# Summing one block's weighted expert rows on the tensor engine throughout, with the next block's expert rows begun earlier

## The chip, the cores and the metric

One Trainium2 chip, one core of it. The metric is the device time of one execution in microseconds. The kernel before was run three times: 1658.19, 1659.23 and 1664.06 us, median 1659.23 us.

## The reference, cut to what matters

512 tokens of 1024 features pass one decoder layer. The mixing sub-layer (sparse attention over a shared latent beside a gated linear recurrence, one output projection, a layer norm) gives `h`. The change is in the second sub-layer, which picks 16 of 16384 single-neuron experts for each of 8 heads, so 128 experts for each token, from the scores of two lists of 128 sub-keys, and sums their rows of `v`:

```python
def one_block(xb):                        # 128 tokens
    q = (xb @ w_q).reshape(PEER_BLOCK, PEER_HEADS, 2, PEER_KEY_DIM // 2)
    s = jnp.einsum('thpd,hpkd->thpk', q, sub_keys)
    s_top, i_top = lax.top_k(s, K)
    ...
    best, pos = lax.top_k(cand.reshape(PEER_BLOCK, PEER_HEADS, K * K), K)
    experts = jnp.take_along_axis(cand_idx.reshape(...), pos, axis=-1)
    g = jax.nn.softmax(best, axis=-1)
    h = jax.nn.gelu(jnp.einsum('td,thkd->thk', xb, u[experts]))
    return jnp.einsum('thk,thkd->td', g * h, v[experts])
```

The result is `LayerNorm(alpha * h + ffn)`. Everything is float32.

## The kernel before, in words

The 512 tokens are four blocks of 128, a token on each partition. **Blocks 2 and 3** are worked densely: all 16384 experts are streamed through the tensor engine, and a matrix `G` holds each token's weight for each expert (zero for most). **Blocks 0 and 1** fetch only the rows that their tokens chose: a "row" here is one indirect DMA that gathers, for each of the 128 tokens, its k-th expert's 1024 features (512 KB, one instruction on the GpSimd queue, `gather`, L625 to L629), and what is then done with it. Each of the two blocks has 128 rows of `u` (a dot product with `h` on VectorE, L651; after every 32 of them a gelu on ScalarE and a product give the weights) and then 128 rows of `v`, which are weighted and summed into the block's tile `hs[b]`.

The program has these stages. `stage([0])` does the mixing layer and the expert choice (`queries`) for block 0. `stage([1, 2, 3])` does the same for the other three blocks: projections (L189, L204), `select` (L416, L417), the recurrence `hgrn` block by block, `attention` block by block, `mix_norm` (L486), `queries` (sub-key scores on TensorE, L518 and L522; the 16 best of each list on VectorE, L532 to L565; `routing`, L567 on, which turns places into expert numbers and weights). Then `dense` builds `G` in 64 steps of four tokens (one-hot tiles on VectorE, L735, and ScalarE, L739; products on TensorE, L744; copies on ScalarE, L722), and loops over 128 groups of experts (`into_hidden`, `weigh`, `out_of_hidden`, L771 and L791).

The rows of blocks 0 and 1 are a background stream. `peer_gather(b)` (L645) is a Python generator that emits one row at each step; `pump(n)` (L693) takes n steps of the first generator in the list `todo`. The stages call `pump` at many places, with the numbers in `PUMP`: in `stage([1, 2, 3])` before 206 rows are asked for, against 204 that the generator of block 0 has. Tile's scheduler then fixes each engine's order when the program is built: it takes what is ready, and among that what comes first in the program. The VectorE instructions of the rows keep their order among themselves. The gathered rows share a ring of four tiles (`GB`).

Block 0's rows of `v` are split. The first 76 are summed on VectorE, each with one instruction that multiplies by the weight and adds to `hs[0]` (L664). The other 52 are summed on TensorE by `pe_gather` (L672 to L688): ScalarE makes a diagonal matrix `dg` of the weights (one tile, L680), two matmuls multiply it with the two halves of the row into two PSUM banks (L682; a float32 matmul shows as two passes, so a row has four), and VectorE adds the banks to `hs[0]` at the end (L687). 14 of the 52 come after the queries of the second stage (`PEK1`), 8 before `G` is built and 30 during its building (`PEK2`, `PEPRE`). Block 1's 256 rows are all on VectorE and begin with the building of `G`: one at every third step (22), the other 234 spread over the 128 groups of the dense loop.

```python
PUMP = {"cw": 4, "qi": 4, "hf": 4, "hq": 4, "hi": 4, "hg": 3, "qa": 2, "hgrn": 1, "att": 4, "mix": 1, "sel": 2,
        "q0": 7, "q1": 0, "q2": 0, "q3": 0}
...
    stage([0], xT0)
    todo.append(peer_gather(0))
    stage([1, 2, 3], consts_loaded["xT1"])
    todo.append(peer_gather(1))
```

Of the kernel before, what the change touches and what calls it, by code (L numbers as in the profile page):

```python
# [24 lines left out]
DENSE = (2, 3)  # L25
# buffers of the rings of tiles
HGB = 5
GB = 4
UB = 4
# [5 lines left out]
# rows of experts worked off at each such place of the program (sel: one at every second step)  # L35
PUMP = {"cw": 4, "qi": 4, "hf": 4, "hq": 4, "hi": 4, "hg": 3, "qa": 2, "hgrn": 1, "att": 4, "mix": 1, "sel": 2,
        "q0": 7, "q1": 0, "q2": 0, "q3": 0}
# rows of block 0's sum that the tensor engine takes: after the queries, and beside the dense weights
PEK1 = 14
PEK2 = 38  # L40
PEPRE = 8
PEG = 60
# tokens of each four whose weights ScalarE multiplies in
GACTS = (3, 4)
# a row of experts at every so manyth group of the dense weights
GPUMP = 3
# the dense step by which all rows are worked off
# [4 lines left out]
def tile_decoder_layer(ctx, tc, a, out):  # L52
# [70 lines left out]
    def layer_norm(ys, os_, g, b, nm):  # L123
        """Each y is a tile or a list of its parts along the features."""
        n = len(ys)
        mv = cst.tile([128, n, 2], F32, name="mv" + nm, tag="ln_mv", bufs=2)
        parts = [y if isinstance(y, list) else [y[:, k * 512:(k + 1) * 512] for k in range(2)] for y in ys]
        for i in range(n):
            st = cst.tile([128, 2, 6], F32, name=f"st{nm}_{i}", tag="ln_st", bufs=2)
            for k in range(2):  # L130
                nc.vector.bn_stats(st[:, k, :], parts[i][k])  # L131
            nc.vector.bn_aggr(mv[:, i, :], st)
        ve = cst.tile([128, n], F32, name="ve" + nm, tag="ln_ve", bufs=2)
        nc.vector.tensor_scalar(ve, mv[:, :, 1], EPS, None, op0=ALU.add)
        r = rsqrt(ve, n, nm)
        for i, o in enumerate(os_):
            if isinstance(ys[i], list):
                for k in range(2):
                    sl = slice(k * 512, k * 512 + 512)
                    nc.vector.scalar_tensor_tensor(o[:, sl], parts[i][k], mv[:, i, 0:1], g[:, sl],  # L140
                                                   op0=ALU.subtract, op1=ALU.mult)
            else:
                nc.vector.scalar_tensor_tensor(o, ys[i], mv[:, i, 0:1], g, op0=ALU.subtract, op1=ALU.mult)  # L143
            nc.vector.scalar_tensor_tensor(o, o, r[:, i:i + 1], b, op0=ALU.mult, op1=ALU.add)  # L144
# [34 lines left out]
    def tok_major(blocks, xT, w, name):  # L179
        """x W for each block, tokens on partitions."""  # L180
        ps_ = [bank(f"{name}{b}") for b in blocks]
        n = w.shape[-1]
        step = 2 if n == 512 else 4
        for k0 in range(0, 8, step):
            wt = stream(f"{name}w{blocks[0]}_{k0}", w[:, k0:k0 + step, :])
            pump(PUMP[name])
            for i in range(len(blocks)):
                for k in range(step):
                    nc.tensor.matmul(ps_[i][:, :n], xT[:, k0 + k, i * 128:(i + 1) * 128], wt[:, k, :],  # L189
                                     start=(k0 + k == 0), stop=(k0 + k == 7))  # L190
        return ps_

    def feat_major(blocks, xT, w, name):
        """(x W)^T for all blocks at once, features on partitions: a bank for each 128 features."""
# [23 lines left out]
    def lower_bound():  # L218
# [7 lines left out]
        # lower bound of the forget gate: f = fa + fc * tanh(z / 2)  # L226
# [42 lines left out]
    def hgrn(b, pr, mixT):  # L269
# [42 lines left out]
        # the states before each chunk of 32  # L312
# [87 lines left out]
    def select(b, pr):  # L400
        """What to add to the negated attention scores of the keys that the index doesn't choose."""
# [91 lines left out]
    def queries(blocks, hT):  # L493
        """Sub-key scores and, for each of the 16 lists, its 16 best."""
# [13 lines left out]
        for g in range(4):  # L508
# [15 lines left out]
            for i, b in enumerate(blocks):  # L524
# [13 lines left out]
                if g >= 2 and i < len(later):  # L538
                    routing(later[i], 0, *r[later[i]])
            if g == 1:  # L540
                later = sorted(blocks, key=lambda b: (b not in DENSE, b))
                if blocks == [0]:
                    routing(later.pop(0), 0, *r[0])
            elif g == 2:
                later = later[len(blocks):]
# [3 lines left out]
    def best16(b, g, sv, si, bv, pos):  # L549
        # a pair (a, b) can be among the 16 best only if (a + 1) * (b + 1) <= 16; the places keep the pairs' order  # L550
# [16 lines left out]
    def routing(b, half, sv, si, bv, pos):  # L567
        """The experts and their weights for four of the block's heads."""
        H = slice(half * 4, half * 4 + 4)
        C = slice(half * 64, half * 64 + 64)  # L570
        # place -> the two ranks
# [22 lines left out]
        # rank -> sub-key  # L594
# [21 lines left out]
        # softmax over the 16 kept, whose first is their maximum  # L616
# [25 lines left out]

    pe_left = list(range(128 - PEK1 - PEK2, 128))

    def peer_gather(b):  # L645
        """Yields True after each row of experts is worked off, False where it waits for pe_gather."""
# [14 lines left out]
        for k in range(128 - (PEK1 + PEK2 if b == 0 else 0)):  # L661
            g = gather(a["v"], b, k, "v")
            tc.keep_in_program_order(
                nc.vector.scalar_tensor_tensor(hs[b], g, gate[:, b, k:k + 1], hs[b], op0=ALU.mult, op1=ALU.add))  # L664
# [4 lines left out]
    weighted = set()  # L669
    spent = set()  # L670

    def pe_gather(n, p):  # L672
        """A part of block 0's sum over the rows of v on the tensor engine: diag(weight) @ rows; yields after each."""
        while 0 not in weighted:
            pump(1)
        ks = [pe_left.pop(0) for _ in range(n)]
        for k in ks:
            g = gather(a["v"], 0, k, "v")
            dg = gat.tile([128, 128], F32, name=f"dg{k}", tag="dg", bufs=1)
            nc.scalar.mul(dg, ident, gate[:, 0, k:k + 1])  # L680
            for i in range(2):
                nc.tensor.matmul(p[i], dg, g[:, i * 512:(i + 1) * 512], start=(k == ks[0]), stop=(k == ks[-1]))  # L682
            if k != ks[-1]:
                yield
        for i in range(2):
            y = hs[0][:, i * 512:(i + 1) * 512]
            nc.vector.tensor_tensor(y, y, p[i], op=ALU.add)  # L687
        yield  # L688

    todo = []  # L690
    rows = [512 - PEK1 - PEK2]
# [10 lines left out]
    def dense(den, dps):  # L702
        """Tokens of the DENSE blocks against every expert, with the experts' weights scattered to a dense matrix."""
# [11 lines left out]
        pw = pe_gather(PEK2, [dps.tile([128, 512], F32, name=f"pw{n}", tag=f"acc0_{n}") for n in range(2)])  # L715
        for _ in range(PEPRE):
            next(pw)
        pdone = PEPRE
# [9 lines left out]
        for t0 in range(0, T, 4):  # L728
# [20 lines left out]
            while pdone < PEK2 and pdone < PEPRE + (t0 // 4 + 1) * (PEK2 - PEPRE) // PEG:  # L749
                next(pw)  # L750
                pdone += 1
# [41 lines left out]
        def residual():  # L793
            ia = gat.tile([128, 128], F32, name="ia", tag="dg", bufs=1)
# [37 lines left out]
    def stage(blocks, xT):  # L832
# [31 lines left out]
        if blocks != [0]:  # L864
# [6 lines left out]
            for _ in pe_gather(PEK1, [bank(f"pv{i}", "hg") for i in range(2)]):  # L871
                pass

    stage([0], xT0)
    todo.append(peer_gather(0))
    stage([1, 2, 3], consts_loaded["xT1"])
    todo.append(peer_gather(1))
# [51 lines left out]
```

## Time and profile before

| what | value |
|---|---|
| median of three runs | 1659.23 us |
| span of the profiled execution, first to last instruction | 1647.0 us |
| TensorE busy (matmuls) | 1456.9 us, 88% |
| TensorE weight loads | 1096.3 us, 67% |
| VectorE busy | 1387.7 us, 84% |
| ScalarE busy | 706.5 us, 43% |
| GpSimd busy | 663.7 us, 40% |
| mean granted TensorE clock | 0.933 |
| DMA | 467.89 MB, mean 284 GB/s |

The page gives the span of the profiled execution, and no time of its own beside it; the median of the runs is 12.2 us above that span, so a change worked out on the span is added to the median. Engine shares are averages over stages whose limits differ: the stage of blocks 1 to 3 lies between about 123 and 745 us, the building of `G` between 745 and 890 us, the dense loop between 890 and 1640 us. A TensorE clock of 1.00 is 2.4 GHz, 0.50 is 1.2 GHz.

### The profile page before, as it was taken

The numbers are of one execution on the slowest core, as the hardware profiler recorded it, in microseconds if no ns is written. First come the engines' busy times: TensorE is split into PE (matmuls) and PEld (weight loads), VectorE is DVE, ScalarE is ACT, GpSimd is POOL, SyncE is SP. The second block draws the span as 40 slices with busy tenths as digits, with TensorE's granted clock in tenths as the row PEclk, the third lists the DMA queues.
The fourth block names the chain that finished last, engine by engine and source line by source line (L and its number), as shares of the span: only waits on it lengthen the run. The fifth ranks groups of instructions, "written<-read, shape, count | busy, mean of one in ns | idle before, by whom it ended". The sixth has DMA issues, their size and how long they took to land. (4 is left out here: it accounts for less than half of the span.)

```text
span 1647.0 us, 24505 instructions
## 1 busy us (share of the span) xinstructions
PE 1456.9 (88%) x7858; PEld 1096.3 (67%) x7858; DVE 1387.7 (84%) x3263; ACT 706.5 (43%) x1501; POOL 663.7 (40%) x531
## 2 busy tenths in 40 slices
PE   8889899763577899868998999999999999999996
PEld 4567444542333365425667888888888889989885
DVE  4139899787787669998887899998999899999998
ACT  3312321122233010327996555555555555555553
POOL 0003423456665251135443344443444345534540
PEclk9899899755599999989999999999999999999998
DMA  7377878788887785246677999999999999999995
GB/s 284 122 275 248 280 265 290 245 273 275 262 276 252 264 306 186 84 136 226 220 218 263 327 345 351 355 345 344 343 356 344 336 347 359 365 349 345 354 358 191
DMA packets 166161, 467.89 MB, mean 284 GB/s; under 512 B 18576, under 2 KB 18704, under 8 KB 165904
## 3 DMA queue, kind: packets, MB, share of 16 engines
q0 software_dynamic: 73728, 268.47, 48.0%
q1 hardware_dynamic: 92304, 197.86, 33.2%
q8 instruction: 62, 1.02, 0.2%
q14 instruction: 67, 0.55, 0.1%
HBM read 464.16 MB, written 2.10 MB: 283 GB/s over the span
## 5 line engine op out<-in xcount | busy, mean ns | idle before, releaser
L627 POOL DMA_INDIRECT gv<-in_v_dram,idx x256 | 335.1, 1309 | 420.0 <-DVE hsA L664 268.6
L627 POOL DMA_INDIRECT gu<-in_u_dram,idx x256 | 318.6, 1245 | 458.2 <-DVE gu L651 289.3
L651 DVE SCALAR_TENSOR_TENSOR gu<-gu,hsA 128x1024 f32<-128x1024 f32 x256 | 309.5, 1225 | 52.5 <-DMA gu<-in_u_dram,idx 51.9
L664 DVE SCALAR_TENSOR_TENSOR hsA<-gv,gate,hsA 128x1024 f32<-128x1024 f32 x204 | 261.6, 1282 | 30.0 <-DMA gv<-in_v_dram,idx 26.6
L760 ACT CAST v_0h<-v 128x512 fp32r<-128x512 f32 x128 | 79.7, 622 | 96.7 <-PE acc L791 55.4
L518 PE MATMUL pq<-hT,wpq 128*128 128x128 f32 (+1 forms) x512 | 118.8, 390 | 0.0
L760 ACT CAST v_1h<-v 128x512 fp32r<-128x512 f32 x128 | 79.5, 621 | 88.6 <-DMA v<-in_v_dram 45.7
L762 DVE TENSOR_TENSOR u_0l<-u,u_0h 128x512 fp32r<-128x512 f32 x128 | 88.5, 692 | 32.7 <-ACT u_0h L760 29.9
L760 ACT CAST u_0h<-u 128x512 fp32r<-128x512 f32 x128 | 79.4, 620 | 72.2 <-PE hp L771 40.1
L791 PE MATMUL acc<-v_0h,wl 128*128 128x512 f32 x256 | 101.9, 398 | 2.5 <-DVE wl L781 2.5
L518 PEld LDWEIGHTS pq<-hT,wpq 128*128 128x128 f32 x512 | 80.0, 198 | 32.1 <-issue 1.7
L762 DVE TENSOR_TENSOR v_1l<-v,v_1h 128x512 fp32r<-128x512 f32 x128 | 87.8, 686 | 15.8 <-ACT v_1h L760 13.5
L791 PE MATMUL acc<-v_0h,wh 128*128 128x512 f32 x256 | 101.0, 394 | 0.0
L791 PE MATMUL acc<-v_1h,wl 128*128 128x512 f32 x256 | 99.7, 389 | 0.0
L791 PE MATMUL acc<-v_1h,wh 128*128 128x512 f32 x256 | 99.7, 389 | 0.0
L791 PE MATMUL acc<-v_0l,wh 128*128 128x512 f32 x256 | 99.5, 390 | 0.0
L760 ACT CAST u_1h<-u 128x512 fp32r<-128x512 f32 x128 | 79.4, 621 | 46.4 <-PE acc L791 42.3
L735 DVE TENSOR_TENSOR og<-iota,dtr 128x512 f32<-128x512 f32 x128 | 81.6, 687 | 13.6 <-PE gb L744 11.7
L762 DVE TENSOR_TENSOR u_1l<-u,u_1h 128x512 fp32r<-128x512 f32 x128 | 87.8, 686 | 5.1 <-ACT wh L779 2.7
L762 DVE TENSOR_TENSOR v_0l<-v,v_0h 128x512 fp32r<-128x512 f32 x128 | 88.0, 688 | 3.4 <-ACT v_0h L760 2.1
L682 PE MATMUL pw<-gv,dg 128*128 128x512 f32 x152 | 76.0, 623 | 15.6 <-ACT dg L680 9.1
L771 PE MATMUL hp<-hTl,u_0h 128*128 128x256 f32 x512 | 84.3, 287 | 5.8 <-ACT u_0h L760 5.8
(282 smaller groups left out, 3166.6 us busy)
## 6 DMA issues: line engine op xcount, KB each, us to landing
v<-in_v_dram SPq DMA_DIRECT2D x256, 256.0 KB
u<-in_ut_dram SPq DMA_DIRECT2D x256, 256.0 KB
wpq<-in_w_pq_dram SPq DMA_DIRECT2D x32, 512.0 KB
wo<-in_w_o_dram SPq DMA_DIRECT2D x16, 512.0 KB
hfw<-in_w_hf_dram SPq DMA_DIRECT2D x8, 512.0 KB
hqw<-in_w_hq_dram SPq DMA_DIRECT2D x8, 512.0 KB
hiw<-in_w_hi_dram SPq DMA_DIRECT2D x8, 512.0 KB
qaw<-in_w_qa_dram SPq DMA_DIRECT2D x8, 512.0 KB
```

What stands on the lines that cost most here:

```text
L518: nc.tensor.matmul(qp[:, :nt], w[:, k, :], hT[:, k, :nt], start=(k == 0), stop=(k == 7))
L627: nc.gpsimd.indirect_dma_start(out=t, out_offset=None, in_=table, in_offset=bass.IndirectOffsetOnAxis(ap=idx[b][k // 64][:, k % 64:k % 64 ...
L651: nc.vector.scalar_tensor_tensor(g, g, 1.0, hs[b], op0=ALU.mult, op1=ALU.mult, accum_out=hd[:, k:k + 1]))
L664: nc.vector.scalar_tensor_tensor(hs[b], g, gate[:, b, k:k + 1], hs[b], op0=ALU.mult, op1=ALU.add))
L682: nc.tensor.matmul(p[i], dg, g[:, i * 512:(i + 1) * 512], start=(k == ks[0]), stop=(k == ks[-1]))
L735: nc.vector.tensor_tensor(og[n], iota[:, None, :].to_broadcast([128, 4, 128]), x[n][:, c:c + 4, None].to_broadcast([128, 4, 128]), op=ALU. ...
L760: nc.scalar.copy(h, x)
L762: nc.vector.tensor_tensor(l, x, h.bitcast(F32), op=ALU.subtract)
L771: nc.tensor.matmul(hp, ut[:, k * 128:(k + 1) * 128], ht[:, n * 4 + k, :], start=(n + q + k == 0), stop=(n == 1 and q == 2 and k == 3))
L791: nc.tensor.matmul(acc[i][n], wt[:, sl], vt, start=(j == 0 and q == 0), stop=(j == 127 and q == 2))
```

## The change

All 128 rows of `v` of block 0 go to TensorE, inside `peer_gather(0)`, in chunks of 16 rows that share two PSUM banks; after each chunk VectorE adds the two banks to `hs[0]`. The banks come from the ring of five with the tag `hg`, which the recurrence, the output projection and the queries also use. `dg` has two tiles (`DGB`) where it had one. `pe_gather` and its constants are gone, from the end of the second stage and from the building of `G`. Block 0's generator is put in the list during its own queries, and `PUMP` now asks for 32 rows there (`q2`, `q3`); in the second stage the numbers for `hgrn`, `qa`, `att` and `mix` rise. Counted by `PUMP`, block 0's 128 rows of `u` end with the projection `hi`, and its rows of `v` run from `hg` through the recurrence and the attention to the middle of `mix_norm`. In the second stage's queries block 1 is routed first, and 32 of its rows of `u` are asked for there; that leaves it 22 rows beside `G` and 202 in the dense loop.

```diff
+DGB = 2
...
-        "q0": 7, "q1": 0, "q2": 0, "q3": 0}
-PEK1 = 14
-PEK2 = 38
-PEPRE = 8
-PEG = 60
+PUMP = {"cw": 4, "qi": 4, "hf": 4, "hq": 4, "hi": 4, "hg": 3, "qa": 3, "hgrn": 2, "att": 6, "mix": 2, "sel": 2,
+        "q0": 6, "q1": 0, "q2": 4, "q3": 4}
+CHUNK = 16
...
@@ queries
-                if g >= 2 and i < len(later):
-                    routing(later[i], 0, *r[later[i]])
+                if g == 2 and b in DENSE:
+                    routing(b, 0, *r[b])
             if g == 1:
-                later = sorted(blocks, key=lambda b: (b not in DENSE, b))
-                if blocks == [0]:
-                    routing(later.pop(0), 0, *r[0])
-            elif g == 2:
-                later = later[len(blocks):]
+                routing(blocks[0], 0, *r[blocks[0]])
+                todo.append(peer_gather(blocks[0]))
...
@@ peer_gather
-        for k in range(128 - (PEK1 + PEK2 if b == 0 else 0)):
+        for k in range(128):
             g = gather(a["v"], b, k, "v")
-            tc.keep_in_program_order(
-                nc.vector.scalar_tensor_tensor(hs[b], g, gate[:, b, k:k + 1], hs[b], op0=ALU.mult, op1=ALU.add))
+            if b == 0:
+                if k % CHUNK == 0:
+                    p = acc_tiles[0](k)
+                dg = gat.tile([128, 128], F32, name=f"dg{k}", tag="dg", bufs=DGB)
+                nc.scalar.mul(dg, ident, gate[:, 0, k:k + 1])
+                for i in range(2):
+                    nc.tensor.matmul(p[i], dg, g[:, i * 512:(i + 1) * 512], start=(k % CHUNK == 0),
+                                     stop=(k % CHUNK == CHUNK - 1))
+                if k % CHUNK == CHUNK - 1:
+                    for i in range(2):
+                        y = hs[0][:, i * 512:(i + 1) * 512]
+                        nc.vector.tensor_tensor(y, y, p[i], op=ALU.add)
+            else:
+                tc.keep_in_program_order(
+                    nc.vector.scalar_tensor_tensor(hs[b], g, gate[:, b, k:k + 1], hs[b], op0=ALU.mult, op1=ALU.add))
...
@@ dense
-            while pdone < PEK2 and pdone < PEPRE + (t0 // 4 + 1) * (PEK2 - PEPRE) // PEG:
-                next(pw)
-                pdone += 1
...
@@ end of stage([1, 2, 3])
-            for _ in pe_gather(PEK1, [bank(f"pv{i}", "hg") for i in range(2)]):
-                pass
+            while 0 not in weighted or (0 not in spent and (rows[0] - 256) % CHUNK):
+                pump(1)
```

## Rows read from the trace of the kernel before

**Rows 1.** Windows: stretch, length, PE PEld DVE ACT POOL busy, clock, DMA share, GB/s
```profile
165.00:290.00 125.00, 114.19 (x295) 54.41 (x293) 112.99 (x262) 30.24 (x54) 45.26 (x45) 0.96 0.80 275
290.00:453.00 163.00, 96.26 (x641) 63.53 (x642) 128.98 (x273) 36.37 (x107) 92.15 (x81) 0.59 0.80 266
453.00:576.00 123.00, 96.92 (x318) 46.79 (x316) 94.07 (x146) 31.29 (x65) 61.72 (x54) 0.93 0.78 265
576.00:682.00 106.00, 99.79 (x365) 63.42 (x365) 91.93 (x439) 22.03 (x42) 29.59 (x27) 0.95 0.55 192
682.00:745.00 63.00, 42.03 (x87) 14.79 (x86) 62.22 (x391) 15.60 (x33) 25.91 (x19) 0.92 0.51 151
745.00:890.00 145.00, 128.00 (x675) 90.44 (x676) 120.72 (x222) 133.85 (x329) 61.42 (x56) 0.96 0.69 222
890.00:1604.00 714.00, 704.55 (x4463) 635.06 (x4461) 658.91 (x1078) 380.37 (x740) 324.48 (x228) 1.00 0.97 348
```

**Rows 2.** Tile gu: min/median/max ns, first and last start us
```profile
L627 POOL DMA_INDIRECT gu<-in_u_dram,idx x256: 932/1150/4955, 141.4 to 1209.0; - x128
L651 DVE SCALAR_TENSOR_TENSOR gu<-gu,hsA x256: 1199/1219/1974, 151.9 to 1218.9; 128x1024 f32<-128x1024 f32 x128
```

**Rows 3.** Windows of tile gu alone: DVE POOL busy, clock, DMA share
```profile
165.00:290.00 125.00, 50.19 (x82) 41.50 (x42) 0.96 0.80 275
290.00:453.00 163.00, 98.19 (x160) 88.66 (x77) 0.59 0.80 266
```

**Rows 4.** Timeline of VectorE where block 0's rows of u end
```profile
451.48 1.22 DVE L651 SCALAR_TENSOR_TENSOR gu<-gu,hsA 128x1024 f32<-128x1024 f32 x1 [0.66 <-DMA gu<-in_u_dram,idx]
...
453.96 1.67 DVE L664 SCALAR_TENSOR_TENSOR hsA<-gv,gate,hsA 128x1024 f32<-128x1024 f32 x1
```

**Rows 5.** Waits between 123 and 745 us: total us, times, longest
```profile
POOL gu L627 <- DVE gu L651: 125.9, 76, 7.1
...
DVE gu L651 <- DMA gu<-in_u_dram,idx: 45.1, 49, 3.4
...
POOL gv L627 <- PE pv L682: 28.0, 12, 11.5
```

**Rows 6.** Groups by form, VectorE and ScalarE, a row of experts
```profile
L651 DVE SCALAR_TENSOR_TENSOR gu<-gu,hsA 128x1024 f32<-128x1024 f32 x256 | 309.5, 1225 | 52.5 <-DMA gu<-in_u_dram,idx 51.9
L664 DVE SCALAR_TENSOR_TENSOR hsA<-gv,gate,hsA 128x1024 f32<-128x1024 f32 x204 | 261.6, 1282 | 30.0 <-DMA gv<-in_v_dram,idx 26.6 <-issue 1.5 <-DVE sv L532 0.4
...
L680 ACT ACTIVATE dg<-ident,gate 128x128 f32<-128x128 f32 x52 | 21.5, 413 | 43.2 <-PE pv L682 26.7 <-PE pw L682 16.2 <-DVE gate L656 0.3
```

**Rows 7.** Groups by line and form: TensorE passes with 512 float32 columns
```profile
L486 PE MATMUL mix<-wo,mixT 128*128 128x512 f32 x128 | 59.2, 622 | 3.7 <-DVE mixT L468 3.7
...
L682 PE MATMUL pw<-gv,dg 128*128 128x512 f32 x152 | 76.0, 623 | 15.6 <-ACT dg L680 9.1 <-DMA gv<-in_v_dram,idx 4.7 <-ACT tab L605 1.6
...
L189 PE MATMUL hq<-hqw,xT 128*128 128x512 f32 x64 | 27.8, 592 | 0.0
```

**Rows 8.** Timeline of TensorE, two rows summed after the queries
```profile
684.47 1.98 PE L682 MATMUL pv<-gv,dg 128*128 128x512 f32 x4 [0.55 <-ACT dg L680]
687.00 1.98 PE L682 MATMUL pv<-gv,dg 128*128 128x512 f32 x4 [0.55 <-ACT dg L680]
```

**Rows 9.** Windows of tile gv alone: PE PEld DVE POOL busy, clock, DMA
```profile
123.00:745.00 622.00, 43.31 (x84) 14.81 (x84) 97.96 (x76) 113.49 (x98) 0.85 0.72 242
```

**Rows 10.** Windows of tile pw alone: PE PEld DVE busy, clock, DMA
```profile
745.00:890.00 145.00, 62.16 (x124) 21.54 (x124) 1.28 (x2) 0.96 0.69 222
```

**Rows 11.** Windows, all engines, where one engine is full (columns of rows 1)
```profile
206.00:247.00 41.00, 41.00 (x97) 18.17 (x96) 39.00 (x105) 9.86 (x13) 11.72 (x12) 1.00 0.76 264
760.00:860.00 100.00, 93.73 (x496) 64.78 (x497) 85.56 (x158) 100.00 (x250) 47.79 (x44) 1.00 0.71 230
```

**Rows 12.** DMA queues of the page: packets, MB, share of 16 engines' span
```profile
q0 software_dynamic: 73728, 268.47, 48.0%
```

**Rows 13.** Tile hsA: the sums added to the block, min/median/max ns
```profile
L687 DVE TENSOR_TENSOR hsA<-hsA,pv x2: 679/682/686, 724.9 to 726.6; 128x512 f32<-128x512 f32 x2
```

More of the change, by code (lines that the diff above doesn't have):

```diff
@@ L34 @@
 PJ = 16
-PUMP = {"cw": 4, "qi": 4, "hf": 4, "hq": 4, "hi": 4, "hg": 3, "qa": 2, "hgrn": 1, "att": 4, "mix": 1, "sel": 2,
-        "q0": 7, "q1": 0, "q2": 0, "q3": 0}
-PEK1 = 14
-PEK2 = 38
-PEPRE = 8
-PEG = 60
+PUMP = {"cw": 4, "qi": 4, "hf": 4, "hq": 4, "hi": 4, "hg": 3, "qa": 3, "hgrn": 2, "att": 6, "mix": 2, "sel": 2,
+        "q0": 6, "q1": 0, "q2": 4, "q3": 4}
+CHUNK = 16
 GACTS = (3, 4)
@@ L641, in finish @@
         nc.sync.dma_start(out[b * 128:(b + 1) * 128, :], hs[b])
-    pe_left = list(range(128 - PEK1 - PEK2, 128))
+    weighted = set()
+    spent = set()
+    acc_tiles = [lambda nm: [bank(f"pv{nm}_{i}", "hg") for i in range(2)]]
     def peer_gather(b):
@@ L667, in peer_gather @@
         spent.add(b)
[L669 to L688, printed above, removed]
     todo = []
-    rows = [512 - PEK1 - PEK2]
+    rows = [512]
     def pump(n):
@@ L714, in dense @@
             tr[b] = [t[:, n, :] for n in range(3)]
-        pw = pe_gather(PEK2, [dps.tile([128, 512], F32, name=f"pw{n}", tag=f"acc0_{n}") for n in range(2)])
-        for _ in range(PEPRE):
-            next(pw)
-        pdone = PEPRE
+        acc_tiles[0] = lambda nm: [dps.tile([128, 512], F32, name=f"pw{nm}_{n}", tag=f"acc0_{n}") for n in range(2)]
         G = den.tile([128, 128, T], F32, name="G")
@@ L748, in dense @@
             pump_some(t0)
-            while pdone < PEK2 and pdone < PEPRE + (t0 // 4 + 1) * (PEK2 - PEPRE) // PEG:
-                next(pw)
-                pdone += 1
         evacuate(T - 4, last)
@@ L793, in residual @@
         def residual():
-            ia = gat.tile([128, 128], F32, name="ia", tag="dg", bufs=1)
+            ia = gat.tile([128, 128], F32, name="ia", tag="dg", bufs=DGB)
             nc.scalar.mul(ia, ident, ALPHA)
@@ L870, in stage @@
                 nc.vector.tensor_tensor(hTl[:, k:k + 2, :], x, hTh[:, k:k + 2, :].bitcast(F32), op=ALU.subtract)
-            for _ in pe_gather(PEK1, [bank(f"pv{i}", "hg") for i in range(2)]):
-                pass
+            while 0 not in weighted or (0 not in spent and (rows[0] - 256) % CHUNK):
+                pump(1)
     stage([0], xT0)
-    todo.append(peer_gather(0))
     stage([1, 2, 3], consts_loaded["xT1"])
-    todo.append(peer_gather(1))
     pre_stack.close()
```

## The prediction

> **What bounds the kernel now.** I read the busy time by stage first, because the shares of the whole span hide four stages with different limits [rows 1]. In the dense loop (890 to 1604 us) TensorE is busy 704.55 of 714 us; nothing that leaves VectorE or the DMA queues there can give back more than the 9.5 us in between. While G is built (745 to 890 us) ScalarE is the limit: 100.00 of 100 us between 760 and 860 us [rows 11]. Between 165 and 682 us no engine is full all the time. What runs there beside the main chain is the stream of rows: block 0's first row of u is gathered at 141.4 us [rows 2], its last is used at 451.48 us, and the first row of v at 453.96 us [rows 4]. The pace was one row in 3.0 us at first (42 gathers in 125 us), then one in 2.1 us (77 in 163 us) [rows 3]. The waits say why it isn't faster: GpSimd waits for VectorE to free a tile of the ring (125.9 us), and VectorE for gathers to land (45.1 us) [rows 5]. Last I read TensorE's room, since the change gives it the work: it idles 67 us of the 163 between 290 and 453 us, at a mean clock of 0.59; 26 of 123 us up to 576; 6 of 106 us up to 682, where the queries of three blocks run; and then, in the 63 us in which VectorE finishes the expert choice (62.22 us busy), its 42 us of work are nearly all rows of v [rows 1, 9].
>
> **The price of a row.** On VectorE a row of v takes 1.28 us [rows 6]. On TensorE it takes four passes of 512 float32 columns. Where such passes follow each other without a break they take 27.8/64 = 0.434 us each, so 1.74 us a row; the diagonal rows now took 76.0/152 = 0.50 us a pass, 2.0 us a row, with the end of the last pass in it [rows 7]. I take 1.85 us, midway, since neighbours on the engine hide a part of that end, and keep 1.74 and 2.0 as bounds. So the change swaps 1.28 us of VectorE for 1.85 us of TensorE, 76 times, and moves 31 further rows (124 passes) from the building of G into the stage before it [rows 10].
>
> **Part 1, rows of v into the second stage.** All 128 now have to be summed before G is built: 128 x 1.85 = 237 us. They can't start at the recurrence, where the program lists them: they follow the rows of u in one stream, and that stream is paced by the ring and the gathers, not by the numbers of PUMP. Starting it during block 0's own queries gains at most the 11 us between the first gather at 141.4 us and the first use at 151.9 us [rows 2], for the gather already follows its indices at once; I count nothing. So the rows of v start near 453 us, as now.
> What is there for them from 453 us on? Idle time of 26 + 6 = 32 us up to 682 us, and 12 us from the clock, which was 0.93 and 0.95 there and would stay at 1.00 (97 x 0.07 + 100 x 0.05) [rows 1]. 237 - 32 - 12 = 193 us are left. Two further places bound the delay of G from both sides. If the last rows lag behind the queries, the 62 us before 745 us, now used by rows that hide there, can be used again. If the main chain's matmuls move ahead into the stretch of the rows of u, 290 to 453 us, they find 67 us of idle time and get 39 us back from the clock (96 us at 0.59), together 106 us. All of both used, and 1.74 us a row: 223 - 44 - 62 - 106 = +11 us. None of it, and 2.0 us a row: 256 - 44 = +212 us. I take half of the 62 us (at 2.1 us a row, 128 rows after 453 us would last until 722 us, so some lag past the queries) and a quarter of the 106 us (the chain's VectorE instructions still stand between rows of u there, so little lets it move): 193 - 31 - 27 = **+135 us**.
>
> **Part 2, what VectorE gets back.** All 76 rows, 98 us, leave it after 453 us [rows 4, 9]. It gets 16 additions of 0.68 us for 8 chunks [rows 13] and 32 rows of u of block 1, 32 x 1.225 = 39 us [rows 6]. Between 453 and 745 us it was busy 248 of 292 us [rows 1], and would be 200: freed, but beside a TensorE that then has more to do than the stretch is long. I count nothing on the path. Cover gone: if the queries came at their old time, those 39 us would stand in the stretch where VectorE is full, and delay G by up to as much; with TensorE late they don't.
> The new wait is the addition after each chunk. Behind it in VectorE's order stand the attention's reductions, and a chunk keeps two banks of the ring of five that recurrence, projection and queries use. The nearest row is the 28.0 us in 12 waits of a gather for such a row's matmul [rows 5], 2.3 us each: 8 chunks, 0 to 19 us. I take 0, as the priced row had one diagonal tile and now there are two, and leave the 19 us to the upper end.
>
> **Part 3, G and the loop.** 31 diagonal matrices of 0.41 us leave ScalarE, which is full there [rows 6, 10, 11]: -13 us. VectorE comes next, 85.56 of 100 us, so the step can fall this far. In the loop 32 rows leave VectorE and the DMA queues; a gather takes 0.480 x 1647 / 512 = 1.54 us of all 16 DMA engines [rows 12], so their share falls from 0.97 by about 0.07, but TensorE's order sets the pace: between 0 and -9.5 us, I take -5 us.
>
> **Sum.** 135 - 13 - 5 = +117 us. The span of 1647.0 us would be 1764 us; the median of the runs lies 12.2 us above the span, so 1776 us. Bounds: 11 - 13 - 9 = -11 us, 1648 us; and 212 - 13 = +199 us, 1858 us (the chunks' 19 us would come on top).
>
> **A rule against this.** Between 206 and 247 us TensorE was busy 41.00 of 41 us with float32 passes, and its weight loads took 18.17 us, 44% [rows 11]: with such passes the engine is full when the loads are under half. The Trainium skill ("Trainium Kernel Development and Optimization", section Performance Expectations) says that matmul busy time is a bad measure of how near a kernel is to the limit, and that the share of LDWEIGHTS is a good one. By that rule TensorE, with 110 us of loads in the 229 us from 453 to 682 us, would be half empty, the rows would fit, and the time would be that of the first rival. I go by the row, which shows a full engine at 44%.
>
> **Rivals.** *TensorE has the room* (faster). Place: 290 to 453 us. If the main chain of blocks 1 to 3, freed of 98 us of VectorE work behind it, takes the idle and half-speed time there, and late rows fill the end, the sum is the lower bound, -11 us: 1648 us, faster by 0.7%. It decides if TensorE is busy over 95% at a clock near 1.00 while rows of u are still gathered. For it: the idle time is there, and VectorE's order holds the chain. Against: rows of u, which hold it in that stretch, stay where they are. Chance 8%. *It cancels*: the same with some 10 us unused, within 8 us of 1659 us; 6%. *Three quarters of it used*: 193 - 62 - 80 - 18 = +33 us, about 1692 us; 8%.
> *TensorE waits for the gathers* (much slower). TensorE runs in order, so a row that hasn't landed, or whose diagonal isn't ready, holds up everything behind it. The rows summed after the queries show that pattern, 2.53 us from row to row [rows 8]. If nothing fits in between, 128 x 2.53 = 324, 324 - 44 - 18 = +262 us: 1921 us. Against: two diagonal tiles, and other work to put between. 8%.
> *It doesn't do what it says*: block 1's rows need indices that are ready only near the end of the queries; if they slip behind the queries, the loop's gain stays and nothing else changes, since they wait for nobody. It is inside the forecast.
>
> **Numbers.** My forecast, with TensorE as the new limit of the second stage, has 70%: 1776 us, its own range 1700 to 1858 us. The range 1678 to 1858 us leaves out the faster and cancelling cases, the waiting case and a little at each end, 2 in 10. About 0.5%, 8 us, is what this kernel's runs can tell from no change. Faster 0.08, same 0.06, slower 0.86 (forecast, three quarters, waiting).
>
> **What would show it.** In the changed profile: last row of u of block 0 near 440 to 455 us; TensorE busy over 95% at clock 1.00 from there to the end of the queries, with 512 passes of diagonal rows in that stretch; the queries' last matmul 100 to 200 us later than 682 us; VectorE with idle time behind TensorE there; steps of G 0.2 us shorter with ScalarE still full; the dense loop within 10 us of its length. I am wrong if the rows of v start before 400 us, if G starts before 780 us, or if TensorE idles between the rows of v while a gather or VectorE is what ends its waits.

## The result, and the profile after

The changed kernel took 1874.89 us (median of 4 runs, 1873.61 to 1876.56), the kernel before beside it 1659.88 us: a ratio of 1.131, interval 1.128 to 1.135. The direction was as forecast; the size was not: 1776 us was said, with 1858 us as the upper end. The profiled execution took 1874.61 us, with a span of 1872.8 us; TensorE was busy 83% of it (before 88%), VectorE 70% (84%), and the DMA queues moved 250 GB/s (284).

The medians lie 215.0 us apart, the two spans 225.8 us. A run of this kernel is listed some 1.7 us above its span, so the profiled execution of the kernel before, with its span of 1647.0 us, was about 10 us shorter than its median run; that much of the 225.8 us is the scatter of one execution. Four places of the two spans say where the 225.8 us lie:

| place | before | after | difference of the step |
|---|---|---|---|
| end of the queries' last sub-key score on TensorE | 682.1 | 888.9 | +206.8 |
| from there to the first product of `G` | 72.3 | 101.4 | +29.1 |
| first to last product of `G` | 131.4 | 128.4 | -3.0 |
| from there to the end | 761.2 | 754.1 | -7.1 |

The windows of the kernel after, cut where its own stages lie (columns as in [rows 1]):

```profile
165.00:290.00 125.00, 117.60 (x305) 56.72 (x304) 112.47 (x250) 28.02 (x51) 57.95 (x56) 0.96 0.90 323
290.00:423.00 133.00, 10.81 (x39) 6.97 (x38) 100.68 (x180) 2.85 (x9) 76.99 (x68) 0.54 0.82 272
423.00:889.00 466.00, 457.23 (x1778) 236.57 (x1778) 143.70 (x660) 133.48 (x331) 122.25 (x131) 0.99 0.55 168
889.00:990.00 101.00, 2.29 (x6) 0.94 (x6) 96.24 (x438) 11.60 (x18) 39.18 (x35) 0.52 0.59 190
990.00:1119.00 129.00, 81.16 (x524) 70.92 (x525) 113.00 (x208) 120.53 (x289) 32.85 (x23) 0.90 0.36 113
1119.00:1833.00 714.00, 706.59 (x4502) 640.76 (x4502) 632.59 (x1012) 387.02 (x748) 299.40 (x196) 1.00 0.93 326
```

Three things are to be seen beside [rows 1]. TensorE, which did 96.26 us of work between 290 and 453 us before, does 10.81 us between 290 and 423 us: 122 us of this stretch are idle, where 67 us were. From 423 to 889 us it is full (457.23 of 466 us, clock 0.99). Then, for 101 us, it does next to nothing (2.29 us) while VectorE is nearly full (96.24 us). The idle time that the change was to fill has moved and grown.

What TensorE waits for in the first stretch, by the waits between 270 and 460 us (total us, times, longest):

```profile
PE pv L666 <- DMA gv<-in_v_dram,idx: 120.7, 5, 118.1
PEld pv L666 <- DMA gv<-in_v_dram,idx: 118.8, 1, 118.8
```

It is one single wait of 118.1 us (the second line is the weight load of the same row). TensorE's timeline shows what stood on both sides of it:

```profile
301.88 2.93 PE L435 MATMUL sp<-ckvT,qlT 128*128 128x256 f32 x6 [0.30 <-ACT qlT L427]
422.92 3.78 PE L666 MATMUL pv<-gv,dg 128*128 128x512 f32 x4 [118.11 <-DMA gv<-in_v_dram,idx]
426.49 1.81 PE L279 MATMUL cum<-lf,tri 128*128 128x512 f32 x2
428.14 1.02 PE L281 MATMUL rev<-lf,tri 128*128 128x512 f32 x2
```

The first row of `v` stands in TensorE's order behind some of the attention's scores and ahead of block 1's recurrence (`cum`, L279). Its gather follows 128 gathers of `u` in the ring, so it lands at 423 us, 1.4 us after the last row of `u` is used (421.55 us; [rows 4] had 451.48). TensorE keeps its order, so block 1's recurrence, which started at 275 us before, waits with it until 426 us.

Later, when rows are there in time, the same order looks like this (TensorE's timeline; behind the start is the time of the group):

```profile
691.68 1.88 PE L666 MATMUL pv<-gv,dg 128*128 128x512 f32 x4
693.39 1.02 PE L435 MATMUL sp<-ckvT,qlT 128*128 128x512 f32 x2
694.25 1.88 PE L666 MATMUL pv<-gv,dg 128*128 128x512 f32 x4
695.97 0.82 PE L447 MATMUL pt<-ident,P 128*128 128x128 f32 x6
```

Nothing waits, and rows stand between the attention's own groups: each row sets the main chain back by its 1.7 us. The groups by form, which answer to [rows 6] and [rows 7]:

```profile
L648 DVE SCALAR_TENSOR_TENSOR gu<-gu,hsA 128x1024 f32<-128x1024 f32 x256 | 312.8, 1231 | 51.4 <-DMA gu<-in_u_dram,idx 50.9
L666 PE MATMUL pv<-gv,dg 128*128 128x512 f32 x512 | 239.7, 604 | 120.9 <-DMA gv<-in_v_dram,idx 120.7
L674 DVE SCALAR_TENSOR_TENSOR hsA<-gv,gate,hsA 128x1024 f32<-128x1024 f32 x128 | 163.5, 1278 | 0.3 <-ACT hsA L657 0.3
L664 ACT ACTIVATE dg<-ident,gate 128x128 f32<-128x128 f32 x128 | 51.3, 401 | 183.6 <-PE pv L666 180.7 <-DVE gate L653 2.5
```

239.7 us for 128 rows are 1.87 us a row. In VectorE's 101 us between the last score and `G`, the windows of tile `gu` alone (DVE, POOL busy, clock, DMA share, GB/s) hold the 32 rows of block 1:

```profile
889.00:990.00 101.00, 39.23 (x64) 39.18 (x35) 0.52 0.59 190
```

And in the building of `G` ScalarE is as full as in [rows 11] and VectorE fuller (92.73 of 100 us, 85.56 there), while TensorE has room (a window in its middle, columns as in [rows 1]):

```profile
1000.00:1100.00 100.00, 64.48 (x436) 55.71 (x436) 92.73 (x172) 99.32 (x239) 22.23 (x16) 0.96 0.32 103
```

### The profile page after: what moved, and what is told of

Read it like the earlier page. It is cut to its first block, busy times and chain, and to the rows that moved or that the text cites. A ratio compares the mean times of both kernels' runs of the same rounds, so it can differ in the third digit from the quotient of the medians.

```text
span 1872.8 us, 25230 instructions
## 1 busy us (share of the span) xinstructions
PE 1548.1 (83%) x8162; PEld 1137.8 (61%) x8162; DVE 1312.6 (70%) x3199; ACT 739.2 (39%) x1575; POOL 647.1 (35%) x531
## 4 chain that ended last, share of the span: by engine, by line
PE 65%; issue 9%; ACT 7%; DVE 7%; POOL 6%; DMA 5%; POOLq 0%; DVEq 0%; SPq 0%; ACTq 0%
PE hp L754 18%; PE acc L774 17%; PE pv L666 11%; PE pq L516 6%; POOL gu L622 6%; PE mix L484 3%; ACT G L708 3%; ACT og L725 3%; DMA gu<-in_u_dram,idx 2%; DMA v<-in_v_dram 2%; DVE gu L648 2%; PE ol L453 1%; PE sp L435 1%; PE psc L520 1%; DMA gv<-in_v_dram,idx 1%
## 5 line engine op out<-in xcount | busy, mean ns | idle before, releaser
L622 POOL DMA_INDIRECT gu<-in_u_dram,idx x256 | 303.0, 1183 | 676.0 <-DVE gu L648 324.5
L666 PE MATMUL pv<-gv,dg 128*128 128x512 f32 x512 | 239.7, 604 | 120.9 <-DMA gv<-in_v_dram,idx 120.7
L666 PEld LDWEIGHTS pv<-gv,dg 128*128 128x128 f32 x512 | 92.7, 191 | 221.4 <-DMA gv<-in_v_dram,idx 118.8
L674 DVE SCALAR_TENSOR_TENSOR hsA<-gv,gate,hsA 128x1024 f32<-128x1024 f32 x128 | 163.5, 1278 | 0.3 <-ACT hsA L657 0.3
L664 ACT ACTIVATE dg<-ident,gate 128x128 f32<-128x128 f32 x128 | 51.3, 401 | 183.6 <-PE pv L666 180.7
L730 PE MATMUL gb<-og,og 128*128 128x128 f32 x512 | 79.2, 307 | 43.8 <-ACT G L708 41.1
L730 PEld LDWEIGHTS gb<-og,og 128*128 128x128 f32 x512 | 68.9, 211 | 54.2 <-ACT G L708 50.5
L774 PE MATMUL acc<-v_0h,wh 128*128 128x512 f32 x256 | 101.4, 396 | 0.0
```

What stands on the lines that cost most here:

```text
L622: nc.gpsimd.indirect_dma_start(out=t, out_offset=None, in_=table, in_offset=bass.IndirectOffsetOnAxis(ap=idx[b][k // 64][:, k % 64:k % 64 ...
L730: nc.tensor.matmul(p[:, tt, :], og[0][:, tt, :], og[1][:, tt, :], start=True, stop=True)
L774: nc.tensor.matmul(acc[i][n], wt[:, sl], vt, start=(j == 0 and q == 0), stop=(j == 127 and q == 2))
```

## The experiments

The theory after the result had three parts: the rows as such are TensorE work that the main chain pays; the parked first row (its matmul waits at the head of TensorE's order, and all behind it waits too) adds to that; the rows of block 1 in the queries add again. Each run takes one of them away, from the kernel after or by putting it into the kernel before. The kernel before ran beside each; its medians were 1652 to 1659 us, so each run is given as a ratio with its 95% interval too.

**The rows of `v` on VectorE** (kernel after; the chunks, the diagonals and their passes are gone, the listing of the rows stays).

```diff
-            if b == 0:
+            if b == 9:
```

> The changed kernel with one thing taken back: all 128 rows of v of block 0 are summed on VectorE again, each with the multiply-and-add of before; order, PUMP and the earlier rows of block 1 stay as in the changed kernel. Theory A (rows on TensorE are the cost: one long wait of 118 us for the first row's gather at the head of TensorE's order, and then 239.7 us of passes in a stretch that is full): block 1's recurrence starts near 275 us again instead of 426 us, the queries' last matmul comes at 700 to 760 us instead of 889 us, the whole takes 1690 to 1740 us. Theory B (the new listing of the rows, with PUMP asking for them earlier, holds up the main chain whatever engine sums them): the recurrence still starts after 400 us and the time stays above 1820 us.

1742.18 us, 1.053 [1.048, 1.057]: 133 us less than the kernel after, 2 us over the end of what was expected. The sums on TensorE, with the parked first row, carry 133 of the 215 us lost; this is net of what the same rows cost the main chain on VectorE. The windows (columns as in [rows 1]) show the old picture, VectorE busy and TensorE with idle time:

```profile
290.00:453.00 163.00, 80.30 (x572) 53.02 (x562) 141.18 (x289) 32.22 (x94) 86.59 (x79) 0.60 0.75 255
453.00:576.00 123.00, 89.14 (x271) 43.19 (x272) 95.81 (x120) 30.40 (x69) 78.27 (x67) 0.82 0.81 277
576.00:682.00 106.00, 65.91 (x205) 37.96 (x204) 76.48 (x104) 10.03 (x19) 56.02 (x48) 0.77 0.86 307
748.00:857.00 109.00, 2.30 (x6) 0.94 (x6) 106.26 (x502) 14.04 (x21) 40.04 (x36) 0.52 0.53 176
```

The rest shows in the places of the spans: the last score ends at 747.9 us (+66 over before), and 52 rows that were on TensorE now stand on VectorE ahead of it, 52 x 1.28 = 67 us; 109 us pass from there to `G` (+37), with block 1's rows in them. `G` and the loop give 9 back.

**The rows listed from the attention on** (kernel after): the parked matmul is gone, and nothing else of the amount of work.

```diff
-"hg": 3, "qa": 3, "hgrn": 2, "att": 6, "mix": 2, "sel": 2,
+"hg": 0, "qa": 0, "hgrn": 0, "att": 11, "mix": 8, "sel": 2,
```

> The changed kernel, with the rows of v listed later in the program: PUMP asks for none at hg, the recurrence and qa, and for all 128 at the attention (11 a place) and the output projection (8 a place). All still run on TensorE. Theory A (the first row's matmul stands in TensorE's order ahead of the recurrence of blocks 1 to 3 and holds it for 118 us, until the rows of u are through): the wait goes, the recurrence starts near 275 us, TensorE does some 60 us of work in the stretch where it idled, and the time falls by 50 to 95 us, to 1780 to 1825 us. Rival (TensorE's sum of work alone sets the end, the wait is filled again later): within 15 us of 1875 us.

1848.72 us, 1.120 [1.114, 1.125]: 26 us. Both expectations missed. Block 1's recurrence does start at 238 us, and TensorE works up to the first row of `v`, which comes at 447.0 us here and at 422.9 us in the kernel after. The windows of this run up to that row, from it to the last score, and of the rows alone in the latter (tile `pv`: PE, PEld, DVE busy, clock, DMA share, GB/s); then the rows alone in the kernel after:

```profile
290.00:447.00 157.00, 78.35 (x546) 52.04 (x547) 130.12 (x279) 31.76 (x94) 81.50 (x70) 0.60 0.71 242
447.00:863.00 416.00, 409.34 (x1214) 201.90 (x1212) 115.09 (x575) 105.40 (x242) 124.47 (x130) 1.00 0.57 186
447.00:863.00 416.00, 233.40 (x512) 93.01 (x512) 10.98 (x16) 1.00 0.57 186
```

```profile
423.00:889.00 466.00, 239.60 (x512) 92.59 (x512) 10.90 (x16) 0.99 0.55 168
```

But the work up to the first row runs at a clock of 0.60. In the kernel after, 78.35 - 10.81 = 67.5 us of it move behind the first row, and there the work other than rows takes only 42 us more (457.23 - 239.60 against 409.34 - 233.40). The rows take 6 us more there, idle time 2 us. That makes the full stretch of the kernel after 50 us longer (466 against 416 us), but it begins 24 us sooner: 50 - 24 = 26. A wait of 118 us was worth 26.

**No rows of block 1 in the queries** (kernel after), and the same rows **in the kernel before** (with block 1 routed first, as the change does it):

```diff
-                pump(PUMP[f"q{g}"])
+                pump(PUMP[f"q{g}"] if blocks == [0] else 0)
```

> The changed kernel without the 32 rows of block 1 in the second stage's queries (they are spread over the dense loop again: 234 rows there); block 1 is still routed first. If those rows are what lengthens the time from the queries' last matmul to the first matmul of G from 72 to 101 us, that time falls back to 70 to 76 us and the loop grows by 2 to 8 us: 1845 to 1855 us. Rival (the routing's order is what lengthens it, since blocks 2 and 3 now come later): still 95 to 105 us there, and no gain.

1847.17 us, 1.117 [1.113, 1.121]: 28 us less than the kernel after, as the theory had it. The stretch from the last score to `G` is 59.6 us, not 101.4, still with a full VectorE, and the loop is 8 us longer:

```profile
889.00:948.00 59.00, 2.30 (x6) 0.94 (x6) 58.21 (x373) 8.66 (x15) 3.17 (x3) 0.53 0.12 40
```

```diff
-        "q0": 7, "q1": 0, "q2": 0, "q3": 0}
+        "q0": 7, "q1": 0, "q2": 4, "q3": 4}
...
+                routing(blocks[0], 0, *r[blocks[0]])
+                if blocks != [0]:
+                    todo.append(peer_gather(1))
```

> The kernel before with only the second part of the change: block 1 routed first, and 32 of its rows of u asked for in the second stage's queries; block 0's rows split between VectorE and TensorE as before. If the 32 rows cost what they take on VectorE where it is full, less what the loop gives back: slower by 20 to 40 us, 1680 to 1700 us. Rival (they fill idle time, as the change means): 1650 to 1660 us.

1700.85 us, 1.028 [1.023, 1.034], some 45 us slower, just over the upper end of what was expected. The queries' last score stays (685.6 us), and `G` starts at 800.5 us, so the stretch between them is 42.6 us longer. Here a second cost comes with the 39 us of VectorE: the 14 last rows of `v` of block 0 are gathered behind block 1's rows in the one ring. The waits between 686 and 800 us, and VectorE's last wait ahead of `G`:

```profile
PE pv L680 <- DMA gv<-in_v_dram,idx: 73.2, 2, 71.6
...
ACT hd L653 <- DVE gu L649: 69.5, 1, 69.5
POOL gu L625 <- DVE dc_m L588: 58.4, 1, 58.4
```

```profile
795.95 0.69 DVE L685 TENSOR_TENSOR hsA<-hsA,pv 128x512 f32<-128x512 f32 x1 [7.78 <-PE pv L680]
```

The rows of `u` wait for their indices (`dc_m` is routing), and the rows of `v` behind them, whose indices had been there for long, wait too. Most of that wait lies beside VectorE's work; 7.8 us of it VectorE waits out at the end. The loop gives nothing back here (765.6 us from the last product of `G` to the end, 761.2 before), although 32 rows left it: block 0's rows beside `G` now end at 953.1 us, 20 us behind its last product, where they ended 15 us ahead of it before.

**Both edits** on the kernel after:

> The changed kernel with two things taken back at once: rows of v listed at the attention and the output projection, and no rows of block 1 in the queries. Alone they gave 26 and 28 us. If they are separate costs (one before the queries' last matmul, one behind it): 1815 to 1830 us. If they are the same one seen twice: 1840 to 1850 us. Either way what is left over the kernel before, 160 us or more, is then the rows' work on TensorE.

1821.20 us, 1.103 [1.098, 1.108]: 54 us, the sum of 26 and 28. What is left, 169 us over the kernel before beside it (1651.96 us), is the rows' work on TensorE: the last score ends at 864.2 us, 182 us later than before, and `G` starts 57.7 us behind it, 15 us less than before.

**Half of the passes** (kernel after; each row adds only one of its two halves, in turn, so half of the sum is left out).

```diff
-                for i in range(2):
+                for i in (k % 2,):
```

> The changed kernel with half of its TensorE passes of rows of v: even rows k add only features 0 to 511, odd ones only 512 to 1023 (the other half of each weighted row is left out of block 0's sum). Gathers, diagonals, banks, order and additions stay. Theory (from 423 to 889 us TensorE is full, 457 of 466 us, so its sum of work sets the end): 256 passes of 0.47 us go, the queries' last matmul comes 100 to 120 us sooner, at 770 to 790 us, and the time is 1755 to 1780 us. Rival (gathers and waits of TensorE's order pace the rows, the passes ride along): the last matmul of the queries stays after 850 us, the time above 1840 us.

1809.02 us, 1.095 [1.091, 1.1]: 66 us, where some 120 us of passes (256 of 0.47 us) were to go, so this missed. From the first row to the last score all of TensorE's work, and that of the rows alone (tile `pv`), took:

```profile
424.00:823.00 399.00, 364.88 (x1522) 190.76 (x1522) 143.21 (x660) 130.61 (x330) 121.10 (x130) 0.96 0.59 196
424.00:823.00 399.00, 139.53 (x256) 43.31 (x256) 10.99 (x16) 0.96 0.59 196
```

In the kernel after these were 457.23 and 239.60 of 466 us. So the rows' work fell by 100 us, not by 120; the other work took 8 us more, and TensorE's idle time grew from 9 to 34 us: 100 - 8 - 25 = 67 us. Most of the idle time lies where the rows are summed, and rows wait for gathers there (window, and the waits in it; the 118.8 us are the wait for the first row):

```profile
424.00:690.00 266.00, 237.58 (x1082) 114.66 (x1082) 60.40 (x160) 106.22 (x285) 119.59 (x128) 0.96 0.76 250
```

```profile
PE pv L666 <- DMA gv<-in_v_dram,idx: 141.3, 28, 118.8
...
POOL gv L622 <- PE pv L666: 118.5, 80, 7.3
```

266 us for 128 rows are 2.1 us from row to row, the pace of the gathers in [rows 3]. That a row at half the price on TensorE meets the gathers as its next limit is a reading of these waits: no run made the gathers faster, and GpSimd for its part waited for TensorE to free tiles of the ring.

**Rows listed into the queries** (kernel after): the last rows of `v` come as late as the program allows, to lag into VectorE's end.

```diff
-"hg": 3, "qa": 3, "hgrn": 2, "att": 6, "mix": 2, "sel": 2,
-        "q0": 6, "q1": 0, "q2": 4, "q3": 4}
+"hg": 0, "qa": 0, "hgrn": 0, "att": 4, "mix": 2, "sel": 2,
+        "q0": 6, "q1": 6, "q2": 5, "q3": 5}
...
-                pump(PUMP[f"q{g}"])
+                pump(PUMP[f"q{g}"] if blocks != [0] else 4)
```

> The changed kernel with block 0's rows listed from the attention on and at lower numbers, so that the last rows of v are listed at the end of the second stage's queries, and with no rows of block 1 there. Theory (TensorE is the limit, and the only idle time left for rows is beside VectorE's end behind the queries): the rows lag behind the queries and fill that end, so G starts 30 to 60 us sooner than the 922 us of the run that listed the rows from the attention on and had no rows of block 1 in the queries (1821 us): 1760 to 1790 us. Rival (the rows are limited by their gathers or by the total of TensorE's work, wherever they are listed): 1815 to 1825 us.

1799.94 us, 1.085 [1.082, 1.088]: 21 us better than with both edits (by the ratios 30 us, as the kernel before took 1658.62 us beside this run and 1651.96 us beside that one), between the two expectations. `G` starts 17 us sooner (905.3 us). TensorE's two windows say why not more (columns as in [rows 1]):

```profile
453.00:850.00 397.00, 388.93 (x1155) 193.21 (x1154) 126.85 (x674) 100.14 (x230) 120.39 (x122) 1.00 0.57 187
...
861.00:905.00 44.00, 10.88 (x26) 4.24 (x24) 43.12 (x261) 10.11 (x19) 4.97 (x6) 0.63 0.26 87
```

The queries themselves were stretched along with the rows (last score 860.8 us, last row 870.1), so only 10.88 us of work lie in the end, where VectorE is full of the expert choice.

**Fewer or more rows on TensorE in the kernel before.** Four runs ask whether a milder form of the change pays: two tiles for `dg`, and the number of rows moved from VectorE to TensorE behind the queries (`PEK1`).

```diff
-PEK1 = 14
+PEK1 = 24
...
-            dg = gat.tile([128, 128], F32, name=f"dg{k}", tag="dg", bufs=1)
+            dg = gat.tile([128, 128], F32, name=f"dg{k}", tag="dg", bufs=2)
```

> The kernel before with two tiles for the diagonal matrix where it has one, nothing else. The rows summed after the queries would follow each other every 1.7 to 1.9 us where they now take 2.53 us. If the end of VectorE's expert choice sets the start of G (62 of 63 us busy), this gives 0 to 6 us: 1650 to 1660 us. If TensorE's rows there set it: 10 to 20 us.

> The kernel before with two tiles for the diagonal and 24 rows instead of 14 on TensorE after the queries, so 66 instead of 76 on VectorE. The 10 rows leave VectorE (12.8 us) just ahead of the expert choice, where it is full from then on, and come to TensorE where it idles. If VectorE sets the start of G there: 6 to 13 us faster than the kernel before, 1643 to 1652 us, faster than both kernels. Rival (the 34 rows of TensorE, at 1.8 us each, now end last): same or slower, 1656 to 1670 us.

> The kernel before with two tiles for the diagonal matrices and 42 instead of 62 of the rows before the expert choice on VectorE (34 more rows allowed on TensorE than on VectorE, instead of 14): ten rows fewer on VectorE than in the run with 24, which took 1643 us. Theory A (VectorE alone still sets when G starts): another 4 to 10 us sooner, 1632 to 1641 us. Theory B (at 1.75 us a row from about 680 us the 42 rows on TensorE now end last): 1645 to 1660 us.

> The kernel before with its one tile for the diagonal matrices and PEK1 at 24 instead of 14, so some 5 rows moved from VectorE to TensorE behind the queries. Theory A (a row on TensorE needs 2.53 us there with one tile, and the moved rows end later than VectorE does): 1655 to 1670 us, and the two tiles are what made the run with 24 faster. Theory B (VectorE's relief alone counts): 1640 to 1648 us, as with two tiles.

By the traces VectorE sums 76 rows of block 0 with `PEK1` at 14, 66 at 24 and 56 at 34; the 62 and 42 rows and the "some 5 rows" of two expectations are miscounts.

| `dg` tiles | `PEK1` | median us | ratio [interval] | rows behind the queries, us | `G` starts | block 1's first row of `u` | from it to the end |
|---|---|---|---|---|---|---|---|
| 1 | 14 (before) | - | 1 | 679.6 to 725.7 | 754.4 | 751.8 | 895.3 |
| 2 | 14 | 1663.84 | 1.007 [1.004, 1.009] | 680.7 to 708.6 | 758.3 | 754.4 | 908.1 |
| 2 | 24 | 1643.42 | 0.995 [0.993, 0.997] | 675.1 to 727.4 | 747.2 | 747.8 | 897.4 |
| 2 | 34 | 1661.53 | 1.002 [0.999, 1.004] | 672.6 to 750.7 | 755.6 | 768.3 | 891.3 |
| 1 | 24 | 1666.24 | 1.007 [1.004, 1.011] | 674.3 to 746.8 | 750.6 | 769.6 | 894.9 |

Two tiles and 24 is faster than the kernel before, by 0.5%: VectorE has fewer rows ahead of the expert choice, and 24 rows fit into TensorE's idle time behind the queries (window of 682 to 745 us, to hold against [rows 1]):

```profile
682.00:745.00 63.00, 51.41 (x111) 20.69 (x110) 59.08 (x355) 18.12 (x40) 31.27 (x27) 0.95 0.68 227
```

With 34 the rows last until 750.7 us, as the theory of a late TensorE had it, and the time is 1.5 us over its range. With one tile and 24 the time is in the range expected of late rows: they last until 746.8 us, 3.0 us each, and TensorE's idle time ahead of them is spent on the one diagonal (tile `pv`, idle until; passes and weight loads are both counted):

```profile
ACT dg L680: 55.7, 42
```

Yet `G` starts sooner there than in the kernel before. What is late is block 1's first row of `u`, by 18 us, and the end comes 894.9 us behind it, near the other rows of the table. That the stream of block 1's rows then sets the end is a reading of these times; no run moved it alone. There is a rival: in this run block 0's rows beside `G` last until 904.5 us, 21 us behind the last product of `G` (before they end at 870.8 us, 15 us ahead of it), so that some of them stand on TensorE between the first groups of the loop, and the loop is 20 us longer (780.9 against 761.2 us). The run with two tiles and 14 rows, a miss, falls out of the pattern (908.1 us), and so does the next run (917.0 us). Why `G` and the loop got longer with two tiles and 14 rows (by 3 and 9 us) stays open.

**More rows of block 1 beside `G`** (the run with two tiles and 24, and every second step instead of every third):

```diff
-GPUMP = 3
+GPUMP = 2
```

> The kernel before with two tiles for the diagonal matrices and PEK1 at 24 (the run that took 0.995 of the kernel before), and beside G a row of block 1 at every second step instead of every third: 32 rows there instead of 22, ten fewer in the dense loop. Theory A (G is bound by ScalarE and VectorE has room for ten rows more; the loop gets shorter by what 32 rows taken out of it gave, 765 - 754 = 11 us, so by 3 us for ten): 0.991 to 0.995 of the kernel before, G as long as in the run with 22. Theory B (VectorE or the gathers then hold up G): G longer by up to 10 x 1.22 = 12 us, 0.996 to 1.003.

1662.04 us, 1.005 [1.002, 1.009], worse than both expectations. `G` takes 150.4 us instead of 133.0. The waits in it, first of this run, then of the run with every third step:

```profile
POOL gu L627 <- PE pw L682: 32.1, 15, 4.6
PEld pw L682 <- DMA gv<-in_v_dram,idx: 24.3, 23, 2.3
PE pw L682 <- DMA gv<-in_v_dram,idx: 19.8, 22, 2.1
```

```profile
POOL gu L627 <- PE pw L682: 8.8, 6, 3.7
PEld pw L682 <- DMA gv<-in_v_dram,idx: 8.1, 10, 2.2
PE pw L682 <- DMA gv<-in_v_dram,idx: 6.6, 10, 2.0
```

The gathers of both blocks share the ring: more of one make the other's late, and TensorE, in its order, waits for each of them ahead of the products of `G`.

## Why the prediction was wrong

**What held.** *The price of a row*: 1.85 us said, 1.87 measured. *The room from 453 us to the end of the queries*: 193 us were to be left of 237; with both extra costs taken out, the last score came 182 us later. TensorE is full there at clock 0.99. The Trainium skill ("Trainium Kernel Development and Optimization", section Performance Expectations) calls MFU (the share of the peak arithmetic) and the share of LDWEIGHTS the good measures of how near a kernel is to the limit. The trace does not agree as to the loads: with 236.57 of 466 us of them, 51%, TensorE had no room left, as the row had it at 44%. The loop gave 7 us where 5 were said. The chunks' waits (50 us in 12) cost nothing that shows, as TensorE stays full meanwhile.

**What failed** is told best by the places. Read by them, the sum had the last score 193 - 31 - 27 = 135 us later, nothing changed in the stretch behind it, `G` 13 and the loop 5 us shorter: +117. Measured: +206.8, +29.1, -3.0, -7.1. The miss of 109 us on the spans is 72 + 29 + 10 - 2. Held against the run with both edits, the 72 are 25 + 16 + 31, all of part 1, and the 29 are 44 - 15, all of part 2.

*Part 1, "a quarter of the 106 us"*: the main chain was to move ahead into 290 to 453 us and win 27 us. It moved back. The sum said that the rows of `v` can't start before the rows of `u` are done, which was right (422.9 us), but made nothing of it that their place in TensorE's order is fixed when the program is built. I had the mechanism in my rivals, as a price for each row; it came as one wait for the first, and its net price is 25 us on the last score (26 us on the time), for the chain's work then runs at a full clock. Without it the chain wins what is left, 193 - 182 = 11 us, not 27.

*Part 1, "half of the 62 us"*: the rows were to lag behind the queries and win 31 us there. They end at 756.5 us, before the queries begin (793.6 us): the rows keep their places among the attention's matmuls, and the queries come behind both. Even the run that lists rows through all the queries has 10.88 us of TensorE work in that stretch.

*Part 2, "I count nothing on the path"*: this was the plainest error. I named the cover, a late TensorE, and it does not cover: behind TensorE's last score VectorE has 57 to 58 us of the expert choice left, even in the runs without those rows. A late TensorE moves this full stretch along with it, and the 32 rows (39 us) stand in it whenever it comes. They make it 44 us longer (101.4 against 57.7 us) and cost 28 us net here, as the loop and `G` give some back; in the kernel before, where the loop gave nothing back, they cost 45 us. What VectorE was freed of was on the path too: with both edits the stretch is 57.7 us where it was 72.3, 15 us won that I had at nothing.

*Part 3*: the 31 diagonals left ScalarE, and `G` got 3 us shorter, not 13. The term was mis-sized. ScalarE's busy time in the stretch fell by 6 us alone (126.75 of 132 us before, 120.53 of 129 us after), and its idle time grew by 3. The window of the kernel before, and ScalarE's groups while `G` is built, first before (754 to 886 us), then after (990 to 1119 us):

```profile
754.00:886.00 132.00, 119.21 (x640) 84.47 (x639) 109.57 (x203) 126.75 (x313) 56.95 (x51) 0.98 0.68 219
```

```profile
L739 ACT ACTIVATE og<-og,dtr 128x128 f32<-128x128 f32 x217 | 71.3, 427 | 0.0
L722 ACT COPY G<-gb 128x512 f32<-128x512 f32 x64 | 66.6, 1087 | 2.4 <-PE gb L744 2.4
L680 ACT ACTIVATE dg<-ident,gate 128x128 f32<-128x128 f32 x29 | 12.2, 422 | 5.1 <-PE pw L682 5.1
```

```profile
L725 ACT ACTIVATE og<-og,dtr 128x128 f32<-128x128 f32 x224 | 69.7, 414 | 1.5 <-DVE og L721 1.5
L708 ACT COPY G<-gb 128x512 f32<-128x512 f32 x63 | 61.7, 1078 | 3.5 <-PE gb L730 3.5
```

Before, these groups sum to 150.1 us, and ScalarE was busy 126.75: the durations overlap, so that 12.2 us of diagonals did not take 12.2 us of the engine's time. After, the two that are left sum to 131.4 us, with 120.53 busy, and seven scalings more (`og`) fall into the stretch. The durations of single instructions on a full engine can't be added up as I did. What ScalarE's added idle time waits for stays open.

The median lies 2 us over the span of the profiled execution, where I had taken 12 from the kernel before; that brought the median 10 us nearer to the forecast, by luck. Of the signs that I named, the 512 passes in a full stretch, the late last score (207 us, a little over my 100 to 200) and the idle VectorE showed; the last row of `u` came at 421.55 us, 18 to 33 us earlier than I had it, and TensorE's idle time ended by a gather lay before the first row, not between rows.

## What to carry to other kernels

Idle time of an in-order engine is worth something only to work that is ready in it at its place in the order: before costing a moved stream at the idle time, find for its first item what it waits for and what is listed behind it. A cover counts only if the covered work does not start from the covering engine's last result. And count a shared ring as a queue: what is put into it early makes what follows in it late, on another engine and in another stage.

## What the runs showed that was not expected

- An idle stretch of 118 us on TensorE cost 26 us, since it took the place of work at a granted clock of 0.60: 67.5 us of this work added 42 us to the stretch at 0.99 that followed.
- With one diagonal tile a row behind the queries took 3.0 us, with two 2.2 us for the same 24 rows (674.3 to 746.8 and 675.1 to 727.4 us), though a diagonal takes ScalarE only 0.4 us.
- Ten rows more beside `G` made its 64 steps 17 us longer while VectorE (122.36 us busy of the 150 us), ScalarE (130.20 us) and the DMA engines (share 0.73) were not full.
